# One triangular inverse for two groups of a head, and a planner that counts returns to dense products

## The chip, the cores and the metric

The kernel runs on one core of a Trainium2 chip. Its time is the device time of one execution in microseconds. Five engines work side by side, each in the order that the program gives it: TensorE (PE, with its weight loads as PEld), VectorE (DVE), ScalarE (ACT), GpSimd (POOL) and SyncE (SP), which issues most DMAs. They wait for each other by semaphores.

## The reference

One step of a two-layer model on a prompt of 2048 tokens and on 8 samples of 8 tokens, width 1024, all in float32. Layer 0 multiplies the input by `w_in_even` and feeds two mixers: a gated delta rule of 4 heads (128 x 128 states) and window attention of 8 heads. Layer 1 multiplies by `w_in_odd` and runs an HGRN2 recurrence of 8 heads. Each layer ends with an output product, a norm and a gated side input (`w_ple_proj`, `w_ple_gate`). What matters here is the delta rule, chunk by chunk:

```python
a_mat = jnp.where(strict, jnp.einsum('nhcid,nhcjd->nhcij', kb, k) * decay, 0.0)
t_inv = lax.linalg.triangular_solve(a_mat + eye, jnp.broadcast_to(eye, a_mat.shape), left_side=True, lower=True)
u = jnp.einsum('nhcij,nhcje->nhcie', t_inv, v * beta[..., None])
w = jnp.einsum('nhcij,nhcjd->nhcid', t_inv, kb * eG[..., None])
```

So each chunk of each head needs the inverse of a unit lower triangular matrix. Then a scan over the chunks carries the state: `v_new = u - w s`, an output, and a new `s`.

## The kernel before, in words

**Work.** The big products (input, output and gate products, called dense here) split each float32 operand into a high and a low part of type float32r and add three products. They have 128 x 128 weights and 256 to 512 columns, and take most of TensorE's time. All else, called side work here, is float32: transposes against the identity, products of 128 x 128, and products on small tiles of the array (32x32, 64x64, 128x32 and so on).

**Layer 0.** The prompt's 16 tiles of 128 tokens are taken in three parts, `GROUPS[0]`: tiles 0-1 (with the samples) and 2-5; 6-9 and 10-11; 12-15. Within a part the work runs head by head (`ORDER`): attention heads and delta heads. For each delta head and each group of tiles, `dense_delta` issues four dense products and starts a `delta_unit`. It computes `delta_core` (norms of keys and queries, decay matrices, the matrix X to be inverted), `inverse`, then the scan, and `rms_out`, which stores the normed output for the output product. A chunk is 128 tokens here, one tile.

**The inverse.** `inverse` works on all tiles of a group at once. Inside the four 32x32 blocks on the diagonal it doubles the size of the inverted blocks in four levels. A level is: VectorE transposes, TensorE multiplies 32x32 tiles (4 a tile of tokens), ScalarE copies the result out of PSUM, TensorE multiplies again, VectorE merges under a mask. Then a join puts the 32-blocks together to 64 (matmuls of one position of the array after the other, for b = 0 and b = 2), and a last one to 128. Each of these steps needs the one before.

**The order.** Every piece of work is a Python generator that yields one instruction at a time. The planner (`Sched.run`, L525) keeps a model clock for each engine; at each turn it takes, of all threads' next instructions, the one that could start first, adds margins (`MARGIN` 700 ns on what TensorE reads) and hands it to its engine. What it writes down is the order on each engine; at run time nothing is reordered. `SWITCH` and `STAY` weigh a change of the array's tile shape: a whole-array matmul is put back by 1000 ns in all while the array is in a small shape. Dense products have the lowest priority of equals (`LATER`) and so fill what the side work leaves. Dense products write three PSUM banks, side work the other five. Since all instructions are recorded in one helper, the profile names line 354 for them all; tiles called `ar` are blocks of on-chip memory, `bank` a PSUM bank, `cst` the constants (the identity among them), `os` the stored outputs. A float32 matmul has two records in the profile, a transpose and a float32r matmul one.

Of the kernel before, what the change touches and what calls it, by code (L numbers as in the profile page):

```python
# [57 lines left out]
SWITCH = {True: 213, False: 100}  # L58
STAY = 1000
# [109 lines left out]
class Op:  # L169
    __slots__ = ("eng", "fn", "cost", "rd", "wr", "tab", "nbytes", "mode", "place", "port")  # L170
# [38 lines left out]
class Sched:  # L209
    def __init__(self, tc):  # L210
        self.tc, self.nc = tc, tc.nc
        self.engines = {e: getattr(tc.nc, e) for e in ("tensor", "vector", "scalar", "gpsimd", "sync")}
        self.clk = dict.fromkeys(self.engines, 0.0)
        self.dma = 0.0
        self.tab = 0
        self.mode, self.place = WHOLE, None
# [131 lines left out]
    def op(self, eng, m, kw):  # L348
# [8 lines left out]
        for k, v in kw.items():  # L357
            if hasattr(v, "ap") and hasattr(v, "offset"):
                if k in ("out", "accum_out", "ap"):
                    wr.append(self.key(v))  # L360
                    if k != "accum_out":
                        out = v
                else:
                    rd.append(self.key(v))
                    if src is None:
                        src = v
        o.rd, o.wr = rd, wr
# [5 lines left out]
        if eng == "tensor":  # L373
# [72 lines left out]
    def emit(self, o, t):  # L446
        o.fn()
        c = o.cost
        if o.eng == "tensor":
            if o.mode == self.mode != WHOLE and o.place != self.place:  # L450
                c = 20 if o.mode[0] == 32 else c / 2 if o.place[1] <= self.place[1] else 14
            self.mode, self.place = o.mode, o.place
# [72 lines left out]
    def run(self):  # L525
        while self.threads:
# [6 lines left out]
            for t in self.threads:  # L533
# [5 lines left out]
                if o.eng == "tensor" and self.mode != o.mode:  # L539
                    s -= SWITCH[o.mode == WHOLE] - STAY * (o.mode == WHOLE)  # L540
# [17 lines left out]
def bank(c="rc"):  # L558
    return Ask("bank", c)
# [18 lines left out]
class Step(Sched):  # L578
    def __init__(self, ctx, tc, a, o):
# [33 lines left out]
        self.xs = {}  # L613
        self.xblocks = 0
# [659 lines left out]
    def delta_core(self, np_, n, cs, q, G4, maskD, small, out, own):  # L1274
# [8 lines left out]
        junk = yield al(128)  # L1283
# [3 lines left out]
        for c in range(n):  # L1287
            yield self.A.activation(out=junk[:np_], in_=psk[:np_, c * 128 : (c + 1) * 128], func=AF.Square, accum_out=ss[:, c : c + 1])
# [3 lines left out]
        for c in range(n):  # L1292
            yield self.A.activation(out=junk[:np_], in_=psq[:np_, c * 128 : (c + 1) * 128], func=AF.Square, accum_out=ss[:, n + c : n + c + 1])
        self.freebank(psq)
        self.free(junk)
# [21 lines left out]
        kdb = yield al(WT)  # L1317
# [38 lines left out]
    def inverse(self, np_, n, cs, X, small):  # L1356


        N = X
        nb, w = np_ // 32, n * 32  # L1360
        rows = [slice(32 * r, 32 * r + 32) for r in range(nb)]
        Db = yield al(w)
        Tb = yield al(w)
        Mb = yield al(w)
        Dv, Tv, Mv = (cut(x[:np_], 32) for x in (Db, Tb, Mb))
        for r in range(nb):
            yield self.V.tensor_tensor(out=Dv[rows[r]], in0=X[rows[r], :, rows[r]], in1=bc(self.c("m1")[rows[r]], 1, n), op=ALU.mult)
        yield self.V.tensor_tensor(out=Dv, in0=Dv, in1=bc(self.c("ident32")[:np_], 1, n), op=ALU.add)
        for s in small[1:] + (None,):
            yield self.V.transpose(out=Tb[:np_], in_=Db[:np_])  # L1370
            if s is None:
                break
            pt = yield bank()
            for c in range(n):
                for r in range(nb):
                    p = rows[r]
                    yield self.P.matmul(out=pt[p, c * 32 : c * 32 + 32], lhsT=X[p, c, p], rhs=Tv[p, c, :], start=True, stop=True)
            yield self.A.activation(out=Mb[:np_], in_=pt[:np_, :w], func=AF.Copy)
            for c in range(n):
                for r in range(nb):  # L1380
                    p = rows[r]
# [3 lines left out]
        for r in range(nb):  # L1385
            yield (self.V.tensor_copy(out=N[rows[r], :, rows[r]], in_=Dv[rows[r]]) if r % 2 else self.A.activation(out=N[rows[r], :, rows[r]], in_=Dv[rows[r]], func=AF.Copy))
        if cs == 128:
            pt = yield bank()
            T2b = yield al(n * 64)
            T2 = cut(T2b[:64], 64)  # L1390
            yield self.G.memset(ap=T2b[:64], constant=0.0)
            for b in (0, 2):
                for c in range(n):
# [4 lines left out]
            for b in (0, 2):  # L1398
                for c in range(n):
                    yield self.P.matmul(out=pt[rows[b], w + c * 32 : w + c * 32 + 32], lhsT=Mv[rows[b + 1], c, :], rhs=Dv[rows[b + 1], c, :], start=True, stop=True)  # L1400
            for c in range(n):
                yield self.P.matmul(out=pt[rows[1], 2 * w + c * 32 : 2 * w + c * 32 + 32], lhsT=Dv[rows[1], c, :], rhs=Mv[rows[1], c, :], start=True, stop=True)
            for b in (0, 2):
                yield self.A.activation(out=N[rows[b], :, rows[b + 1]], in_=cut(pt[rows[b], w : 2 * w], 32), func=AF.Copy)
            yield self.V.tensor_copy(out=T2[rows[1], :, 0:32], in_=cut(pt[rows[1], 2 * w : 3 * w], 32))
            self.freebank(pt)
            M2b = yield al(n * 64)
            M2 = cut(M2b[64:128], 64)
            pt = yield bank()
            for c in range(n):  # L1410
                yield self.P.matmul(out=pt[64:128, c * 64 : c * 64 + 64], lhsT=X[0:64, c, 64:128], rhs=T2[:, c, :], start=True, stop=True)
            yield self.A.activation(out=M2b[64:128], in_=pt[64:128, : n * 64], func=AF.Copy)
            for c in range(n):
                yield self.P.matmul(out=pt[0:64, n * 64 + c * 64 : n * 64 + c * 64 + 64], lhsT=M2[:, c, :], rhs=N[64:128, c, 64:128], start=True, stop=True)
            yield self.V.tensor_copy(out=N[0:64, :, 64:128], in_=cut(pt[0:64, n * 64 : 2 * n * 64], 64))
# [4 lines left out]
    def delta_unit(self, half, h, gi, u):  # L1420
# [7 lines left out]
        yield from self.delta_core(128, nt, 128, u["c"], (G[:, sl, h], GmB[:, sl, h], GrB[:, sl, h]), self.c("maskD"), SMALL, r, True)  # L1428
# [36 lines left out]
    def rms_out(self, np_, n, cs, po, lqk, g, sg, dst):  # L1465


        sm = yield al(256)
        f, junk = sm[:np_, 128 : 128 + n], sm[:np_, 0:128]
        for c in range(n):  # L1470
            yield self.A.activation(out=junk, in_=po[:np_, c * 128 : (c + 1) * 128], func=AF.Square, accum_out=f[:, c : c + 1])
# [6 lines left out]
        on = yield al(n * 128)  # L1478
# [237 lines left out]
    def hgrn_core(self, np_, n, cs, q, k, f, deep, out, own):  # L1716
# [14 lines left out]
        def scale(s):  # L1731
# [6 lines left out]
            yield self.V.tensor_tensor(out=qv[:, :, 1, :], in0=qv[:, :, 1, :], in1=bc(bv[:, :, 0], 2, hs), op=ALU.mult)  # L1738
            yield self.V.tensor_tensor(out=kv[:, :, 0, :], in0=kv[:, :, 0, :], in1=bc(bv[:, :, 1], 2, hs), op=ALU.mult)
# [3 lines left out]
            bo += nbk  # L1743
            yield self.V.tensor_tensor(out=B, in0=bv[:, :, 0], in1=bv[:, :, 1], op=ALU.mult)

# [62 lines left out]
        if deep:  # L1808
# [19 lines left out]
            for i, s in enumerate((4, 8, 16)):  # L1828
                yield from level(ps, i * n * 16, s)
            self.freebank(ps)  # L1830
            yield from scale(64)
# [362 lines left out]
```

## Time and profile before

| | |
|---|---|
| median of 3 runs | 3127.14 us (3126.95 to 3135.73) |
| profiled execution | 3119.46 us |
| its span, first to last instruction | 3117.7 us |
| TensorE busy | 3002.6 us (96%) |
| VectorE, ScalarE, GpSimd busy | 1964.8, 1228.3, 198.7 us |
| TensorE idle, ended by VectorE, by ScalarE | 54.3 us, 48.0 us |
| mean granted TensorE clock | 0.983 |
| HBM traffic | 78 GB/s over the span |

The busy time of an engine is the union of its instructions' times. Of TensorE's rows the starts are used, since a matmul's end overlaps the next one's. The span and what lies around it make the profiled execution's own time, which is 7.7 us under the median of the other runs.

### The profile page before, as it was taken

The page shows a single profiled execution, that of the slowest core. Times are in us where ns is not written, and L with a number is a line of the kernel's source. Part 1 is how long each engine was busy: PE and PEld are TensorE (multiplying, and loading weights), DVE is VectorE, ACT ScalarE, POOL GpSimd, SP SyncE. Part 2 cuts the span into 40 slices and gives each one's busy share as a digit, 9 for nine tenths or more (in the row PEclk, how much of TensorE's full clock was granted, in tenths as well). Part 3 has the DMA queues.
Part 4 walks back from the last instruction along what each step waited for, and adds up shares of the span by engine and source line. Part 5 has one row for each costly group of instructions (what it writes and reads, how often), then busy time and mean ns, then how long its engine had stood idle before and what let it go on. Part 6 is the DMA issues. An engine that isn't in the chain of part 4 may idle for free. (4 is left out here: it accounts for less than half of the span.)

```text
span 3117.7 us, 63598 instructions
## 1 busy us (share of the span) xinstructions
PE 3002.6 (96%) x25592; PEld 2498.8 (80%) x25592; DVE 1964.8 (63%) x5693; ACT 1228.3 (39%) x3314; POOL 198.7 (6%) x265
## 2 busy tenths in 40 slices
PE   8999999999999999999999999998999999999999
PEld 7887778877787787878888888887888888787787
DVE  5567776786767675333367786868577677733333
ACT  4555555564556462101144343434444444411011
POOL 0000000000000001111100000000000000111110
PEclk9999999999999999999999999999999999999999
DMA  4221132231214154333332121222221122732331
GB/s 119 71 77 47 47 92 63 71 80 44 68 54 114 48 171 138 87 79 88 88 112 64 49 63 49 76 64 87 70 59 56 44 70 61 213 87 75 83 86 49
DMA packets 320838, 246.45 MB, mean 79 GB/s; under 512 B 33800, under 2 KB 285840, under 8 KB 320528
## 3 DMA queue, kind: packets, MB, share of 16 engines
q1 hardware_dynamic: 253408, 207.80, 22.0%
q0 software_dynamic: 67136, 34.61, 6.2%
q8 instruction: 200, 3.28, 0.4%
q14 instruction: 94, 0.77, 0.1%
HBM read 182.98 MB, written 60.45 MB: 78 GB/s over the span
## 5 line engine op out<-in xcount | busy, mean ns | idle before, releaser
L354 PE MATMUL bank<-ar,ar 128*128 128x512 f32 (+10 forms) x20432 | 2813.2, 302 | 67.2 <-ACT ar L354 39.8
L354 PEld LDWEIGHTS bank<-ar,ar 128*128 128x128 f32 (+4 forms) x20432 | 2244.8, 162 | 474.2 <-ACT ar L354 65.1
L354 ACT ACTIVATE ar<-bank 128x128 f32<-128x128 f32 (+13 forms) x1471 | 525.9, 368 | 1081.5 <-PE bank L354 998.6
L354 DVE TENSOR_TENSOR ar<-ar,ar 128x256 f32<-128x256 f32 (+8 forms) x1500 | 732.6, 517 | 247.9 <-ACT ar L354 210.3
L354 ACT ACTIVATE ar<-ar 128x512 f32<-128x512 f32 (+15 forms) x1067 | 527.8, 522 | 750.0 <-DVE ar L354 384.6
L354 DVE SCALAR_TENSOR_TENSOR ar<-ar,bank 128x512 f32<-128x512 f32 (+3 forms) x256 | 164.1, 641 | 386.6 <-ACT ar L354 254.2
L354 PE MATMUL bank<-cst,ar 128*128 128x128 f32 (+3 forms) x1439 | 239.7, 279 | 27.5 <-DVE ar L354 16.4
L354 PEld LDWEIGHTS bank<-cst,ar 128*128 128x128 f32 (+3 forms) x1439 | 173.5, 141 | 73.8 <-DVE ar L354 16.9
L354 POOL TENSOR_TENSOR ar<-ar,mhalf 128x2 f32<-128x2 f32 (+3 forms) x104 | 109.2, 1050 | 1496.8 <-DVE ar L354 1130.1
L354 DVE TENSOR_TENSOR ar<-bank,ar 128x128 fp32r<-128x128 f32 (+7 forms) x326 | 147.2, 455 | 75.7 <-ACT ar L354 43.7
L354 DVE TENSOR_TENSOR ar<-ar 128x4 f32<-128x4 f32 (+10 forms) x592 | 139.9, 250 | 19.9 <-ACT ar L354 13.3
L354 DVE SCALAR_TENSOR_TENSOR ar<-bank,ar,ar 128x509 f32<-128x509 f32 (+8 forms) x216 | 122.7, 573 | 25.8 <-ACT ar L354 24.4
L354 DVE SCALAR_TENSOR_TENSOR ar<-ar,ar,bank 128x128 f32<-128x128 f32 x192 | 65.8, 343 | 115.2 <-PE bank L354 114.6
L354 PEld LDWEIGHTS bank<-ar 32*32 32x32 f32 (+3 forms) x2640 | 88.8, 121 | 38.9 <-ACT ar L354 13.6
L354 PE MATMUL bank<-ar 32*32 32x32 f32 (+5 forms) x2640 | 113.7, 209 | 4.5 <-ACT ar L354 2.3
L354 DVE COPY_PREDICATED ar<-cst,bank 128x64 f32<-128x64 uint32 (+3 forms) x356 | 85.9, 242 | 34.9 <-PE bank L354 24.4
L354 DVE SCALAR_TENSOR_TENSOR ar<-ar,ar,ar 128x1024 f32<-128x1024 f32 (+1 forms) x68 | 87.0, 1280 | 13.8 <-POOL ar L354 13.8
L354 POOL MEMSET ar<- 128x256 f32 (+4 forms) x85 | 29.1, 348 | 961.1 <-PE bank L354 550.6
L354 DVE SCALAR_TENSOR_TENSOR ar<-ar,ar 128x4 f32<-128x4 f32 (+10 forms) x190 | 58.4, 312 | 31.7 <-ACT ar L354 30.5
L354 POOL DMA_DIRECT2D ar<-os x64 | 57.3, 898 | 296.9 <-PE bank L354 197.0
L354 ACT ACTIVATION_READ_ACCUMULATOR ar<-bank 128x1 f32 (+1 forms) x340 | 66.2, 195 | 0.0
L354 ACT ACT_TABLE_LOAD x49 | 62.9, 1283 | 5.5 <-DVE ar L354 4.0
(55 smaller groups left out, 799.9 us busy)
## 6 DMA issues: line engine op xcount, KB each, us to landing
ar<-os POOLq DMA_DIRECT2D x64, 512.0 KB, 5.0
ar<-in_w_in_odd SPq DMA_DIRECT2D x64, 512.0 KB
ar<-in_w_in_even SPq DMA_DIRECT2D x60, 512.0 KB
os<-ar SPq DMA_DIRECT2D x36, 512.0 KB
ar<-x SPq DMA_DIRECT2D x32, 512.0 KB
os<-ar SPq DMA_DIRECT2D x56, 256.0 KB
ar<-in_x_prompt SPq DMA_DIRECT2D x16, 512.0 KB
ar<-in_w_ple_gate SPq DMA_DIRECT2D x16, 512.0 KB
```

The lines of the kernel that those rows point to most:

```text
L354: o.fn = lambda: f(**kw)
```

## The change

It has four parts.

- **The meeting.** Where a part has two groups, the unit of the first group that has its X waits (in the planner, as a condition of its generator) until the second has its own; that one's thread then runs one `inverse` over the tiles of both and lets the first go on. With 2 and 4 tiles a phase has 24 small matmuls instead of 8 and 16.
- **The join** issues the matmuls of both halves (b = 0 and 2) before the two ScalarE copies, and in turn by position; results that went to three stretches of the bank go to two.
- **The planner** counts 90 ns for the first dense product behind anything else (`BACK`), puts a dense product back by 300 ns when the last instruction on TensorE was other whole-array work, and by 900 ns in all (before, 1000) when the array is in a small shape.
- **Scrap results apart.** The squares on ScalarE, of which only the sums are used, write to separate columns of a tile that is filled later. In layer 1 the scalings and the merges under masks are recorded in turn.

```diff
-SWITCH = {True: 213, False: 100}
-STAY = 1000
+SWITCH = {True: 105, False: 120}
+BACK = 90
+STAY = (900, 300)
...
+            o.dense = o.mode == WHOLE and m != "transpose" and kw["rhs"].dtype == F32R
...
+            if o.dense and not self.was_dense:
+                c += BACK
+            self.mode, self.place, self.was_dense = o.mode, o.place, o.dense
...
-                if o.eng == "tensor" and self.mode != o.mode:
-                    s -= SWITCH[o.mode == WHOLE] - STAY * (o.mode == WHOLE)
+                if o.eng == "tensor":
+                    if self.mode != o.mode:
+                        s -= SWITCH[o.mode == WHOLE] - STAY[0] * (o.mode == WHOLE)
+                    elif o.dense and not self.was_dense:
+                        s += STAY[1]
...
-        yield from self.inverse(np_, n, cs, X, small)
+        if own:
+            yield from self.meet(own, X, np_, cs, small)
+        else:
+            yield from self.inverse(np_, cs, [X], small)
...
+    def meet(self, own, X, np_, cs, small):
+
+        m = self.met.setdefault(own, [])
+        m.append(X)
+        if len(m) < len(GROUPS[0][own[0]]):
+            yield until(lambda: own not in self.met)
+            return
+        yield from self.inverse(np_, cs, m, small)
+        del self.met[own]
+        self.dirty = True
...
+            for c, (X, i) in enumerate(at):
+                for b in (0, 2):
+                    yield self.P.matmul(out=pt[rows[b + 1], c * 32 : c * 32 + 32], lhsT=X[rows[b], i, rows[b + 1]], rhs=Tv[rows[b], c, :], start=True, stop=True)
             for b in (0, 2):
-                for c in range(n):
-                    yield self.P.matmul(out=pt[rows[b + 1], c * 32 : c * 32 + 32], lhsT=X[rows[b], c, rows[b + 1]], rhs=Tv[rows[b], c, :], start=True, stop=True)
-                yield self.A.activation(out=Mb[rows[b + 1]], in_=pt[rows[b + 1], :w], func=AF.Copy)
+                yield self.A.activation(out=Mb[rows[b + 1], :w], in_=pt[rows[b + 1], :w], func=AF.Copy)
...
-            yield self.A.activation(out=junk, in_=po[:np_, c * 128 : (c + 1) * 128], func=AF.Square, accum_out=f[:, c : c + 1])
+            yield self.A.activation(out=on[:np_, c * 128 : (c + 1) * 128], in_=po[:np_, c * 128 : (c + 1) * 128], func=AF.Square, accum_out=f[:, c : c + 1])
```

How it moves the instructions, at two places on TensorE. First a level of the first delta head's inverse: its two phases on 32x32 tiles and what stands between them. Before, for the group of two tiles (`bank_73` takes the small results, `bank_68` a dense product's):

```order
L354 MATMUL bank_73<-ar_2203,ar_1790 32x32 x8
L354 MATMUL bank_68<-ar_123,ar_2016 128x320
L354 MATMUL bank_68<-ar_124,ar_2015 128x320
L354 MATMUL bank_68<-ar_127,ar_2015 128x320
L354 MATMUL bank_68<-ar_124,ar_2016 128x320
L354 MATMUL bank_68<-ar_124,ar_2015 128x320
L354 MATMUL bank_68<-ar_127,ar_2015 128x320
L354 MATMUL bank_68<-ar_124,ar_2016 128x320
L354 MATMUL bank_73<-ar_2203 32x32 x8
```

Of the change, for both groups (`bank_70` takes the small results; `ar_118` and `ar_2415` are the two groups' X):

```order
L355 MATMUL bank_70<-ar_2312,ar_118 32x32 x8
L355 MATMUL bank_70<-ar_2312,ar_2415 32x32 x16
L355 MATMUL bank_67<-ar_182,ar_1911 128x512
L355 MATMUL bank_67<-ar_183,ar_1910 128x512
L355 MATMUL bank_67<-ar_187,ar_1910 128x512
L355 MATMUL bank_67<-ar_183,ar_1911 128x512
L355 MATMUL bank_67<-ar_183,ar_1910 128x512
L355 MATMUL bank_70<-ar_2312 32x32 x24
```

The 8 and 16 small matmuls of two levels now stand together, with five dense products of 512 columns between the phases where seven of 320 stood.

Second the join's first step, with the semaphores that each row waits for. Before, for a group of four tiles: half b = 0, half b = 2, then dense products, then the second step:

```order
L354 MATMUL bank_71<-ar_2432,ar_2522 32x32 [waits DVE_49]
L354 MATMUL bank_71<-ar_2432,ar_2522 32x32 x3
L354 MATMUL bank_71<-ar_2432,ar_2522 32x32 [waits Activation_49]
L354 MATMUL bank_71<-ar_2432,ar_2522 32x32 x3
L354 MATMUL bank_68<-ar_181,ar_2016 128x512
L354 MATMUL bank_68<-ar_182,ar_2015 128x512
L354 MATMUL bank_68<-ar_186,ar_2015 128x512
L354 MATMUL bank_68<-ar_182,ar_2016 128x512
L354 MATMUL bank_68<-ar_182,ar_2015 128x512
L354 MATMUL bank_71<-ar_2359,ar_2432 32x32 [waits Activation_49]
```

Of the change, for both groups together, up to the first dense products:

```order
L355 MATMUL bank_69<-ar_2312,ar_118 32x32 [waits DVE_49]
L355 MATMUL bank_69<-ar_2312,ar_118 32x32 x3
L355 MATMUL bank_69<-ar_2312,ar_2415 32x32 x8
L355 MATMUL bank_68<-ar_184,ar_1951 128x512
L355 MATMUL bank_68<-ar_188,ar_1951 128x512
L355 MATMUL bank_68<-ar_184,ar_1952 128x512
L355 MATMUL bank_66<-ar_181,ar_2217 128x512
```

The wait for ScalarE between the halves is gone: the twelve matmuls stand together, and the next row that waits for ScalarE is the second step, 16 dense products later.

More of the change, by code (lines that the diff above doesn't have):

```diff
@@ L169 @@
 class Op:
-    __slots__ = ("eng", "fn", "cost", "rd", "wr", "tab", "nbytes", "mode", "place", "port")
+    __slots__ = ("eng", "fn", "cost", "rd", "wr", "tab", "nbytes", "mode", "place", "port", "dense")
 class Ask:
@@ L215, in __init__ @@
         self.tab = 0
-        self.mode, self.place = WHOLE, None
+        self.mode, self.place, self.was_dense = WHOLE, None, True
         self.port = 0.0
@@ L613, in __init__ @@
         self.xs = {}
+        self.met = {}
         self.xblocks = 0
@@ L1364, in inverse @@
         Mb = yield al(w)
[L1365 to L1367 removed]
+        Dv, Tv, Mv = (cut(x[:np_, :w], 32) for x in (Db, Tb, Mb))
+        for X, g in groups:
+            for r in range(nb):
+                yield self.V.tensor_tensor(out=Dv[rows[r], g], in0=X[rows[r], :, rows[r]], in1=bc(self.c("m1")[rows[r]], 1, g.stop - g.start), op=ALU.mult)
         yield self.V.tensor_tensor(out=Dv, in0=Dv, in1=bc(self.c("ident32")[:np_], 1, n), op=ALU.add)
         for s in small[1:] + (None,):
[L1370 removed]
+            yield self.V.transpose(out=Tb[:np_, :w], in_=Db[:np_, :w])
             if s is None:
@@ L1373, in inverse @@
             pt = yield bank()
+            for c, (X, i) in enumerate(at):
+                for p in rows:
+                    yield self.P.matmul(out=pt[p, c * 32 : c * 32 + 32], lhsT=X[p, i, p], rhs=Tv[p, c, :], start=True, stop=True)
+            yield self.A.activation(out=Mb[:np_, :w], in_=pt[:np_, :w], func=AF.Copy)
             for c in range(n):
[L1375 to L1378, printed above, removed]
-            for c in range(n):
-                for r in range(nb):
-                    p = rows[r]
+                for p in rows:
                     yield self.P.matmul(out=pt[p, w + c * 32 : w + c * 32 + 32], lhsT=Mv[p, c, :], rhs=Dv[p, c, :], start=True, stop=True)
@@ L1396, in inverse @@
+        if cs == 128:
             for r in range(2):
                 yield self.V.tensor_copy(out=T2[rows[r], :, rows[r]], in_=Tv[rows[r]])
-            for b in (0, 2):
-                for c in range(n):
-                    yield self.P.matmul(out=pt[rows[b], w + c * 32 : w + c * 32 + 32], lhsT=Mv[rows[b + 1], c, :], rhs=Dv[rows[b + 1], c, :], start=True, stop=True)
             for c in range(n):
-                yield self.P.matmul(out=pt[rows[1], 2 * w + c * 32 : 2 * w + c * 32 + 32], lhsT=Dv[rows[1], c, :], rhs=Mv[rows[1], c, :], start=True, stop=True)
@@ L1403, in inverse @@
-            for b in (0, 2):
-                yield self.A.activation(out=N[rows[b], :, rows[b + 1]], in_=cut(pt[rows[b], w : 2 * w], 32), func=AF.Copy)
-            yield self.V.tensor_copy(out=T2[rows[1], :, 0:32], in_=cut(pt[rows[1], 2 * w : 3 * w], 32))
+                k = slice(w + c * 32, w + c * 32 + 32)
+                for b in (0, 2):
+                    yield self.P.matmul(out=pt[rows[b], k], lhsT=Mv[rows[b + 1], c, :], rhs=Dv[rows[b + 1], c, :], start=True, stop=True)
+                yield self.P.matmul(out=pt[rows[1], k], lhsT=Dv[rows[1], c, :], rhs=Mv[rows[1], c, :], start=True, stop=True)
@@ L1406, in inverse @@
+            pv = cut(pt[:, w : 2 * w], 32)
+            yield self.V.tensor_copy(out=T2[rows[1], :, 0:32], in_=pv[rows[1]])
+            for X, g in groups:
+                for b in (0, 2):
+                    yield self.A.activation(out=X[rows[b], :, rows[b + 1]], in_=pv[rows[b], g], func=AF.Copy)
             self.freebank(pt)
             M2b = yield al(n * 64)
-            M2 = cut(M2b[64:128], 64)
+            M2 = cut(M2b[64:128, : n * 64], 64)
             pt = yield bank()
-            for c in range(n):
-                yield self.P.matmul(out=pt[64:128, c * 64 : c * 64 + 64], lhsT=X[0:64, c, 64:128], rhs=T2[:, c, :], start=True, stop=True)
@@ L1412, in inverse @@
[L1412 to L1415, printed above, removed]
+            for c, (X, i) in enumerate(at):
+                yield self.P.matmul(out=pt[64:128, c * 64 : c * 64 + 64], lhsT=X[0:64, i, 64:128], rhs=T2[:, c, :], start=True, stop=True)
@@ L1416, in inverse @@
+            yield self.A.activation(out=M2b[64:128, : n * 64], in_=pt[64:128, : n * 64], func=AF.Copy)
+            for c, (X, i) in enumerate(at):
+                yield self.P.matmul(out=pt[0:64, c * 64 : c * 64 + 64], lhsT=M2[:, c, :], rhs=X[64:128, i, 64:128], start=True, stop=True)
+            for X, g in groups:
+                yield self.V.tensor_copy(out=X[0:64, :, 64:128], in_=cut(pt[0:64, : n * 64], 64)[:, g])
             self.freebank(pt)
```

53 lines of the change are left out of this document (30 added, 23 removed).

## The prediction

> **What bounds the kernel now.** I read the page first, its busy times and its slices.
>
> ```profile
> span 3117.7 us, 63598 instructions
> PE 3002.6 (96%) x25592; PEld 2498.8 (80%) x25592; DVE 1964.8 (63%) x5693; ACT 1228.3 (39%) x3314; POOL 198.7 (6%) x265
> PE   8999999999999999999999999998999999999999
> PEclk9999999999999999999999999999999999999999
> ```
>
> TensorE is busy for 96% of the span in every slice but two; no other engine comes near. So a gain must come out of TensorE's own time: fewer or cheaper matmuls, less lost between them, or part of the 115 us in which it is idle. The windows by stage, and the waits of TensorE, say where the idle time is (columns of the windows: length, then busy time and instructions of each engine, granted clock, DMA share, GB/s).
>
> ```profile
> 0.00:1143.00 1143.00, 1072.54 (x10732) 883.43 (x10732) 787.71 (x2621) 619.58 (x1745) 32.02 (x62) 0.97 0.27 76
> 1143.00:1600.00 457.00, 452.33 (x2128) 365.93 (x2124) 206.13 (x359) 83.79 (x176) 50.21 (x48) 1.00 0.40 105
> 2180.00:2205.00 25.00, 20.04 (x118) 15.39 (x117) 12.64 (x45) 9.37 (x36) 1.25 (x2) 0.73 0.45 139
> PE bank L354 <- DVE ar L354: 54.3, 92, 3.1
> PE bank L354 <- ACT ar L354: 48.0, 46, 7.3
> ```
>
> The first 1143 us, where attention and the delta rule run beside layer 0's input products, hold 70 of the 115 us. The change works in that stretch.
>
> **What a switch of TensorE costs.** The number of matmuls of each shape is the same in both programs (19,344 in all, counted in both orders), so the products themselves give nothing. What changes is who stands beside whom. I took the price of a neighbour from the timeline of TensorE, by the starts, because the ends overlap. First, transposes between dense products of 128x512:
>
> ```profile
> 1213.95 0.60 PE L354 MATMUL bank<-cst,ar 128*128 128x128 f32 x4
> 1214.31 1.40 PE L354 MATMUL bank<-ar,ar 128*128 128x512 f32 x5
> 1215.54 0.60 PE L354 MATMUL bank<-cst,ar 128*128 128x128 f32 x4
> 1215.90 23.65 PE L354 MATMUL bank<-ar,ar 128*128 128x512 f32 x103
> 1239.38 0.60 PE L354 MATMUL bank<-cst,ar 128*128 128x128 f32 x4
> ...
> 103.74 1.25 PE L354 MATMUL bank<-cst,ar 128*128 128x128 f32 x10
> 104.75 0.77 PE L354 MATMUL bank<-ar,ar 128*128 128x384 f32 x3
> ```
>
> 103 dense matmuls take 23.48 us from start to start and 5 take 1.23, so one takes 0.227 and the return to dense adds 0.095. But four transposes take 0.36 and ten 1.01: one takes 0.108, four should take 0.43, and 0.07 is given back, since the last one is followed early. A return from transposes, and likewise from whole-array float32 products, costs some 0.02 us net. That is not the 90 ns that the changed planner charges as BACK.
>
> Small tiles are another matter:
>
> ```profile
> 677.85 0.45 PE L354 MATMUL bank<-ar 32*32 32x32 f32 x32 [0.20 <-DVE ar L354]
> 678.24 1.42 PE L354 MATMUL bank<-ar,ar 128*128 128x512 f32 x5
> 679.59 0.45 PE L354 MATMUL bank<-ar 32*32 32x32 f32 x32
> 679.97 1.65 PE L354 MATMUL bank<-ar,ar 128*128 128x512 f32 x6
> ...
> 239.16 0.33 PE L354 MATMUL bank<-ar 32*32 32x32 f32 x16
> 239.42 1.29 PE L354 MATMUL bank<-ar,ar 128*128 128x320 f32 x7
> ```
>
> Each float32 matmul has two records. The 5 dense ones between two small phases take 1.35 us, 0.215 over 5 x 0.227. A phase of 16 small matmuls takes 0.38, one of 8 takes 0.26: 0.016 a matmul and 0.13 fixed. **An excursion from dense to small tiles and back costs 0.215 + 0.13 = 0.345 us besides its matmuls.**
>
> **The change part by part.**
>
> *One inverse for two groups.* Layer 0's part 0 and part 1 have two groups a head, part 2 has one. So 20 inverses over groups of 2 or 4 tiles become 12 (eight of 6 tiles, four of 4), and the two of the samples stay. Over the whole order, excursions away from the whole array fall from 430 to 352, runs of 32x32 from 199 to 124: 78 x 0.345 = **-27 us**.
>
> *Positions in turn.* In the join of the 32-blocks the order before issues the matmuls of all tiles at one position of the array, then those of the next; now positions alternate.
>
> ```profile
> 281.23 0.43 PE L354 MATMUL bank<-ar,ar 32*32 32x32 f32 x8
> 748.46 0.21 PE L354 MATMUL bank<-ar,ar 32*32 32x32 f32 x1 [3.09 <-ACT ar L354]
> ```
>
> Four at one position take 0.43 with their tail, as long as the sixteen above (0.45); the tail alone is 0.21. That is 0.055 each against 0.016. The order before has 221 neighbours at one position, the changed one none: 221 x 0.04 = **-9 us**.
>
> These rows give -36. As a second way I took the median distance from start to start for each kind of neighbours (the shape before, the shape, the shape behind) over all of TensorE's records, and summed it along both orders: 2919 us before, 2870 after, **-49**. The rest of the second sum is dense matmuls that stood alone between other work (116 before, 6 now) and switches from one small shape to another. The lower bound is -27, were the positions hidden and the rest nothing. I take **-48**, near the finer count.
>
> *The wait inside the join goes.* ScalarE's rows of two such places, with TensorE's, and the groups of 32x32 matmuls (columns: busy, mean ns, idle before and what ended it):
>
> ```profile
> 745.85 1.28 ACT L354 ACT_TABLE_LOAD   x1
> 747.14 0.30 ACT L354 ACTIVATE ar<-ar,eps 128x4 f32<-128x4 f32 x1
> 747.43 0.69 ACT L354 ACTIVATE ar<-bank,ar 128x512 f32<-128x512 f32 x1
> 748.14 0.27 ACT L354 ACTIVATE ar<-bank 32x128 f32<-32x128 f32 x1
> ...
> 283.15 1.32 PE L354 MATMUL bank<-ar,ar 32*32 32x32 f32 x11 [1.49 <-ACT ar L354]
> 283.62 0.27 ACT L354 ACTIVATE ar<-bank 32x128 f32<-32x128 f32 x1 [0.52 <-PE bank L354]
> ...
> L354 PE MATMUL bank<-ar,ar 32*32 32x32 f32 x3752 | 75.8, 196 | 29.5 <-ACT ar L354 20.8 <-DVE ar L354 8.6
> L354 PE MATMUL bank<-ar 32*32 32x32 f32 x1048 | 20.0, 198 | 2.3 <-ACT ar L354 1.7 <-DVE ar L354 0.2
> ```
>
> The second half of the first join writes the bank that ScalarE still reads for the first half, and nothing stands between the halves. At 748.46 TensorE had waited 3.09 us, because ScalarE had a table load and two other instructions to do first. I count 18 such places, 22 us together, which are nearly all of the 20.8 + 1.7 that ScalarE ended in these groups. Now both halves come first and both copies behind them, with dense work until the next phase: **-22 us**. Next in line is ScalarE's copy for the second phase; if its cover failed, as many waits of 0.5 to 1 us would be back in 12 places, 6 to 12 us.
>
> *New waits.* The rule that charges 300 for a return from other whole-array work makes the planner take a side matmul that is up to 0.3 us late, so its margin of 0.7 us shrinks to 0.4. I priced the TensorE work between the cause of each awaited ScalarE or VectorE result and its user, by the same medians. Before, 24 uses have under 0.4 us of it (the joins and a few more), now 4. Between 0.4 and 1.1 us there are 32 before and 62 now. In the run before those 32 lost 7 us together, 0.22 each; 30 more are **+5 us**, a little less than 30 x 0.22, as most of them lie above 0.9. The bounds: 0, and +41, were each of 136 returns 0.3 us late (returns to dense fall from 1014 to 800, of which 78 are the excursions above).
>
> *At nothing.* The meeting is a condition of the planner: no engine waits in it. The first group's scan, norm and store are only recorded later, on SP's queue too; their reader is the output product behind the last head. ScalarE loses 56 copies, VectorE some 100 small instructions; at 39% and 63% they are hidden, as are the squares that now write apart and the other order of scalings in layer 1. If the cover were gone, they would count as gains.
>
> Sum: -48 - 22 + 5 = **-65 us**, so 3119.46 becomes 3054 for a profiled execution. The profiled one lies 7.7 us under the median of the runs, 3127.14: **3062 us**.
>
> **The rivals.**
>
> *Phases exposed (slower).* Two inverses that ran side by side covered each other's round trips; one inverse has 8 + 3 of them, 132 in the 12. From 283.15 to the end of ScalarE's copy at 283.89 is 0.74 us. All exposed they are +98, so 3160; from 88 exposed on nothing is gained, from about 100 it is slower. For it: one place of the changed order has only four whole-array products between two phases. Against it: most have four to ten dense ones of 0.227.
>
> *Clock (slower).* The granted clock is 1.00 where dense products run through and 0.73 in the window at 2180, where mixed work and waits stand. Over the span 0.017 of the clock is missing, 53 us; the clock records have it in 16 stretches at half clock, so 6.6 us long on average, each losing 3.3.
>
> ```profile
> core 0: 3117.7 us, clock 0.983
> ```
>
> By the order, stretches over 2 us without a dense product rise from 20 to 43. If each of the 23 new ones brought a half-clock stretch it would cost 23 x 3.3 = 76 us: 3138. Against it: those over 3.4 us rise only from 7 to 10, which would be 10 us. The Trainium skill ("TensorE: Matmul & The Clock Gate", Part 4: PE-mode transpose) says that transposes do not count as activity for the clock, which speaks against bunching them. The trace fits it at 2180 and cannot tell it from the waits there.
>
> *Only the wait goes (faster, less).* The excursions' price is won on TensorE and lost to later results, since the planner's durations and the chip's differ and each reordering finds new late ones: 3127 - 22 - 10 = 3095, to 3115.
>
> *More.* Fewer waits also mean less of the 53 us of missing clock, and the uses that had 1.5 us and more of cover fall too: another 15 to 30, so 3040.
>
> **How the numbers follow.** Forecast (3040 to 3085) 0.60; more (under 3040) 0.15; only the wait (3085 to 3117) 0.17; phases exposed 0.04; clock 0.04. The range of 8 in 10 leaves out the slower cases and the best tail: 3035 to 3100. A change within 0.3% (9 us) can't be told from none; of the 0.08 of the two slower cases 0.03 ends there: faster 0.92, same 0.03, slower 0.05.
>
> **What would show it.** In the changed profile: the row of 32x32 matmuls with under 10 us ended by ScalarE instead of 20.8; TensorE's idle time in layer 0 down from 70 to about 50; excursions at the same 0.345; the clock at 0.98. It is wrong if waits for VectorE or ScalarE before whole-array matmuls grow by over 30 us, or if the granted clock falls to 0.96.

## The result and the profile after

The changed kernel takes **3048.68 us** (median of 4 runs, 3046.65 to 3053.54) against 3127.05 us for the kernel before: ratio 0.9746, 95% interval 0.9724 to 0.9767. Forecast were 3062 us and a range of 3035 to 3100. The profiled execution took 3046.65 us, its span 3044.4 us.

The page of the changed kernel, its busy times and clock slices:

```profile
span 3044.4 us, 63289 instructions
PE 2947.7 (97%) x25592; PEld 2477.3 (81%) x25592; DVE 1947.0 (64%) x5589; ACT 1202.0 (39%) x3258; POOL 195.6 (6%) x257
PEclk9989999999999999999999999998999999999999
```

Its clock, in the view of the cores:

```profile
core 0: 3044.4 us, clock 0.987
```

TensorE has the same 25592 records and 54.9 us less busy time; the span is 73.3 us shorter. The windows of layer 0 (columns as before: length, busy time and instructions of PE, PEld, DVE, ACT, POOL, clock, DMA share, GB/s), cut where its part on 32x32 tiles now ends:

```profile
0.00:1090.00 1090.00, 1033.78 (x10766) 867.96 (x10766) 778.23 (x2538) 601.04 (x1696) 30.61 (x54) 0.98 0.29 79
1090.00:1540.00 450.00, 446.76 (x2077) 361.42 (x2076) 199.37 (x334) 78.66 (x164) 51.08 (x48) 1.00 0.40 106
```

TensorE is idle for 56.2 us there, where it was 70.5 us in the longer window before (about 50 was expected). The waits of TensorE, and its two groups of 32x32 matmuls:

```profile
PE bank L355 <- DVE ar L355: 53.1, 81, 5.1
PE bank L355 <- ACT ar L355: 20.0, 19, 7.5
PE bank L355 <- DMA ar<-x: 10.2, 2, 5.5
```

```profile
L355 PE MATMUL bank<-ar,ar 32*32 32x32 f32 x3860 | 55.5, 195 | 7.7 <-DVE ar L355 5.5 <-ACT ar L355 1.3 <-DVE halo L355 0.6
L355 PE MATMUL bank<-ar 32*32 32x32 f32 x940 | 15.3, 194 | 1.9 <-issue 1.9
```

What ScalarE ended fell from 48.0 to 20.0 us; of the 20.8 + 1.7 us before 32x32 matmuls 1.3 are left. Neither VectorE's waits nor the clock got worse; the two waits for a load of x grew, from 4.5 to 10.2 us, and some 3 us of small waits are new.

The price of an excursion is what it was. TensorE's timeline in layer 0's last part, then two rows from an earlier place:

```profile
948.34 0.45 PE L355 MATMUL bank<-ar 32*32 32x32 f32 x32
948.73 1.65 PE L355 MATMUL bank<-ar,ar 128*128 128x512 f32 x6
950.22 0.60 PE L355 MATMUL bank<-cst,ar 128*128 128x128 f32 x4
...
952.57 1.18 PE L355 MATMUL bank<-ar,ar 128*128 128x512 f32 x4
953.67 0.45 PE L355 MATMUL bank<-ar 32*32 32x32 f32 x32
...
679.05 0.62 PE L355 MATMUL bank<-ar,ar 32*32 32x32 f32 x48
679.60 0.44 PE L355 MATMUL bank<-cst,ar 128*128 128x128 f32 x2
```

Sixteen small matmuls take 0.39 us from start to start and six dense ones behind them 1.49, which is 0.13 over 6 x 0.227: the way back. On the way out, four dense ones between transposes and a small phase take 1.10, 0.19 over 4 x 0.227, of which 0.095 is the return from the transposes. Together that is 0.225, where the prediction had 0.215. (Over all stretches of 128x512 products between two small phases, without waits and at full clock, the median is 0.226 now and 0.223 before.) A phase for both groups, 24 matmuls (48 records), takes 0.55: with the same fixed 0.13, 0.0175 a matmul.

**Where the time went.** I set the start-to-start medians of the kernel before, by kind of neighbours, against the starts of the changed one. TensorE's first to last start went from 3104.5 to 3029.9 us. Of these 74.6 us, 49.4 are neighbours (2919.3 to 2869.9) and 25.3 what lies over the medians (185.2 to 159.9). The first of these is counted along the order with the old medians, as in the prediction; only the total is measured. By place: layer 1's scan begins 55.4 us earlier, as the first of its 128x16 matmuls shows, before and after:

```profile
1640.51 0.45 PE L354 MATMUL bank<-ar 128*32 128x16 f32 x32
```

```profile
1585.10 0.44 PE L355 MATMUL bank<-ar 128*32 128x16 f32 x32
```

From there to its last such matmul it takes 1019.5 us instead of 1032.4, and the rest 432.8 instead of 438.9.

### The profile page after: what moved, and what is told of

The parts are those of the page before. It is cut to its first block, busy times and chain, and to the rows that moved or that the text cites. A ratio compares the mean times of both kernels' runs of the same rounds, so it can differ in the third digit from the quotient of the medians.

```text
span 3044.4 us, 63289 instructions
## 1 busy us (share of the span) xinstructions
PE 2947.7 (97%) x25592; PEld 2477.3 (81%) x25592; DVE 1947.0 (64%) x5589; ACT 1202.0 (39%) x3258; POOL 195.6 (6%) x257
## 5 line engine op out<-in xcount | busy, mean ns | idle before, releaser
L355 PE MATMUL bank<-ar,ar 128*128 128x512 f32 (+9 forms) x20370 | 2752.3, 300 | 59.3 <-DVE ar L355 37.4
L355 PEld LDWEIGHTS bank<-ar,ar 128*128 128x128 f32 (+3 forms) x20370 | 2227.1, 161 | 436.6 <-issue 53.8
L355 ACT ACTIVATE ar<-bank 128x128 f32<-128x128 f32 (+12 forms) x1415 | 514.3, 378 | 1105.5 <-PE bank L355 1027.0
L355 DVE TENSOR_TENSOR ar<-ar,ar 128x128 f32<-128x128 f32 (+11 forms) x1494 | 748.8, 520 | 247.2 <-ACT ar L355 204.2
L355 ACT ACTIVATE ar<-ar 128x256 f32<-128x256 f32 (+12 forms) x1061 | 527.5, 524 | 669.4 <-DVE ar L355 309.9
L355 PE MATMUL bank<-cst,ar 128*128 128x128 f32 (+2 forms) x1439 | 236.0, 280 | 21.7 <-DVE ar L355 10.4
L355 PEld LDWEIGHTS bank<-cst,ar 128*128 128x128 f32 (+2 forms) x1439 | 171.7, 141 | 68.0 <-DVE ar L355 14.4
L355 POOL TENSOR_TENSOR ar<-ar,mhalf 128x2 f32<-128x2 f32 (+4 forms) x104 | 106.7, 1026 | 1586.3 <-DVE ar L355 1140.2
L355 DVE TENSOR_TENSOR ar<-ar 128x128 f32<-128x128 f32 (+9 forms) x598 | 139.3, 248 | 18.1 <-ACT ar L355 14.7
L355 PEld LDWEIGHTS bank<-ar 128*32 128x32 f32 (+3 forms) x2702 | 86.0, 120 | 30.1 <-issue 16.4
```

Of the source, the lines that this page charges most:

```text
L355: o.fn = lambda: f(**kw)
```

## The experiments

"Start of layer 1" is the time of that first 128x16 matmul in the profiled execution, "scan" the length of its stage, "neighbours" the sum of the old medians along the order, and "over" what TensorE's time from first to last start has beyond that sum. Each ratio is against runs of the kernel before in the same session, whose medians lie between 3125.62 and 3132.48 us.

| kernel | median us | ratio (95%) | start of layer 1 | scan | neighbours | over |
|---|---|---|---|---|---|---|
| before | 3127.05 | 1 | 1640.5 | 1032.4 | 2919 | 185 |
| the change | 3048.68 | 0.9746 (0.9724 to 0.9767) | 1585.1 | 1019.5 | 2870 | 160 |
| the change, again | 3053.15 | 0.9754 (0.9734 to 0.9773) | 1588.5 | 1024.1 | 2870 | 168 |
| new join alone | 3100.39 | 0.9911 (0.9896 to 0.9926) | 1620.9 | 1034.0 | 2908 | 180 |
| planner alone | 3133.11 | 1.0011 (0.9995 to 1.0027) | 1638.2 | 1045.8 | 2916 | 195 |
| planner of before | 3078.77 | 0.9837 (0.9819 to 0.9855) | 1591.3 | 1042.3 | 2872 | 191 |
| no meeting | 3086.99 | 0.9866 (0.9847 to 0.9884) | 1625.0 | 1025.2 | 2902 | 175 |
| returns free | 3042.90 | 0.9732 (0.9716 to 0.9749) | 1573.7 | 1026.6 | 2871 | 157 |
| old first join step | 3071.42 | 0.9820 (0.9803 to 0.9837) | 1606.0 | 1023.4 | 2875 | 180 |
| scrap, layer 1 as before | 3086.41 | 0.9869 (0.9852 to 0.9886) | 1609.4 | 1036.7 | 2877 | 194 |
| scrap alone as before | 3073.44 | 0.9822 (0.9802 to 0.9841) | 1603.6 | 1027.1 | 2874 | 182 |
| margin 720 | 3063.62 | 0.9796 (0.9779 to 0.9813) | 1585.5 | 1035.9 | 2872 | 175 |
| leaving free | 3105.12 | 0.9919 (0.9903 to 0.9936) | 1603.8 | 1056.8 | 2906 | 179 |
| leaving at 2000 | 3197.35 | 1.0209 (1.0189 to 1.0229) | 1710.7 | 1034.7 | 2838 | 335 |

### The join

The kernel before with the new `inverse` for one group, nothing else:

```diff
-        yield from self.inverse(np_, n, cs, X, small)
+        yield from self.inverse(np_, cs, [X], small)
```

> The kernel before with the new join alone: both halves of the first step ahead of the two copies, positions in turn; every group keeps its own inverse, the planner and all else are as before. Theory (TensorE's time is the sum of neighbour prices plus the waits that have no cover): the neighbour sum along this order is 2908 us against 2919 (positions, -9), and uses with under 0.4 us of cover fall from 24 to 5, worth 22 us. So about 3092 us, -35, and the 32x32 groups lose under 5 us to ScalarE instead of 22. Rival 'excursions carry it all, the waits come back elsewhere': 3115 to 3120.

27 us, 8 fewer than the theory and nearer to it than to the rival. The 32x32 groups lose 3.2 us to ScalarE, as expected. Its waits of TensorE:

```profile
PE bank L354 <- DVE ar L354: 61.5, 91, 3.3
PE bank L354 <- ACT ar L354: 33.1, 31, 7.4
```

ScalarE's fell by 14.9 us from 48.0, and VectorE's rose by 7.2 from 54.3: about half of the wait that went came back as another. The reverse, the change with the old first step of the join:

```diff
             for b in (0, 2):
+                for c, (X, i) in enumerate(at):
+                    yield self.P.matmul(out=pt[rows[b + 1], c * 32 : c * 32 + 32], lhsT=X[rows[b], i, rows[b + 1]], rhs=Tv[rows[b], c, :], start=True, stop=True)
                 yield self.A.activation(out=Mb[rows[b + 1], :w], in_=pt[rows[b + 1], :w], func=AF.Copy)
```

> The changed kernel with the first step of the join as before: the matmuls of one half, ScalarE's copy, then the other half; meeting, planner, scrap and layer 1 as changed. So 12 merged inverses wait again in their join (16 uses under 0.4 us of cover instead of 4), and the matmuls of a half stand at one position (104 such neighbours instead of 0; neighbour sum 2875 against 2870). Theory: 12 x 1.2 us = +14 and +5, layer 1 as in the changed kernel, since the order there is the same: 3066 to 3070, and the first small matmul of layer 1 at 1600 to 1605. Rival 'the wait is hidden, since VectorE's next result is late anyway': 3049 to 3056.

It costs 23 us, nearly all ahead of layer 1 (1606.0 against 1585.1). In its profile part of the wait is back, in what ScalarE ended in all and before the 32x32 group:

```profile
PE bank L355 <- ACT ar L355: 31.2, 31, 7.6
L355 PE MATMUL bank<-ar,ar 32*32 32x32 f32 x4340 | 68.8, 196 | 14.0 <-ACT ar L355 8.5 <-DVE ar L355 4.0 <-DVE halo L355 0.6
```

By TensorE's starts the two halves stand apart in twelve places again, by 0.61 to 1.64 us, 9 us together where the theory had 14. With the 5 of the neighbours that is 14 of the 23; the rest was not traced.

### The meeting

```diff
-        if own:
-            yield from self.meet(own, X, np_, cs, small)
-        else:
-            yield from self.inverse(np_, cs, [X], small)
+        yield from self.inverse(np_, cs, [X], small)
```

> The changed kernel in which each group keeps its own inverse (20 instead of 12); join, planner, scrap and layer 1 as changed. Excursions 435 instead of 352, neighbour sum 2902 against 2870, waits without cover the same (5 and 4 uses under 0.4 us). Theory: 31 us slower than the changed kernel, 3080. Rival 'the waits in the join were the gain and merging only moves work': 3049 to 3055. Rival of the other sign 'merging exposes phases': under 3049.

38 us are lost, and layer 1 starts 40 us later: the meeting is the largest part. The profiled executions lie 46 apart; of that the neighbours give 31 (435 excursions instead of 352) and what lies over the medians 15.

### The planner's numbers

Two kernels: the one before with the new numbers and rules alone, and the change with the old numbers. The diff is the second's:

```diff
-SWITCH = {True: 105, False: 120}
-BACK = 90
-STAY = (900, 300)
+SWITCH = {True: 213, False: 100}
+BACK = 0
+STAY = (1000, 0)
```

> The kernel before with the planner's new numbers and rules alone (SWITCH, BACK, STAY); inverses, join and all else as before. Returns to dense fall from 1014 to 876, excursions to small tiles stay at 434 (430 before). Theory: a return from whole-array side work costs 0.02 us net, so 138 fewer give 3 us; the neighbour sum along this order is 2916 against 2919; five waits less in joins by chance. 3117 to 3127. Rival 'each return costs the 90 ns that the planner charges': -12 from the returns beside that, so 3105 to 3115.

> The changed kernel with the planner's numbers and rules of before (returns to dense cost nothing there, small shapes are held as before); meeting, join, scrap and layer 1 as changed. Returns to dense 930 instead of 800, excursions 365 instead of 352, neighbour sum 2872 against 2870 of the changed kernel. Theory: 3050 to 3057, within 0.3% of the changed kernel's 3049. Rival '90 ns a return': 130 x 0.09 = +12, 3060 or more.

Alone they are worth nothing (1.0011, interval across 1). With the meeting, the old numbers gave 3078.77, 30 us over the change, where 3050 to 3057 was expected: a miss. But up to layer 1, where the meeting is, only 6 us differ; 23 stand in layer 1's scan. Is that the numbers' doing, or that of any other order? Two more orders tell. One changes only the margin on what TensorE reads (`MARGIN = 720` instead of 700):

> The changed kernel with one number of the planner moved a little: MARGIN 720 instead of 700. It means nothing by itself and gives another order, so it measures what a new order alone does. Neighbour sum 2872 against 2870; 6 uses under 0.4 us against 4, 38 under 1.1 against 62. Theory: within 10 us of the changed kernel up to layer 1 (1575 to 1595) and within 20 in all, 3040 to 3070. If it lies over 3070, single comparisons of 20 us between orders say nothing.

Layer 1 starts at the same time and its scan is 16 us longer. So a change of 20 ns in a margin, which means nothing by itself, moves that stage by 16 of those 23 us, and the 30 us say little about the numbers. The other lets the returns go free:

```diff
-BACK = 90
-STAY = (900, 300)
+BACK = 0
+STAY = (900, 0)
```

> The changed kernel in which the planner counts nothing for a return to dense from whole-array side work (BACK 0, second STAY 0); its other numbers and all else as changed. Returns to dense rise from 800 to 940, excursions stay (354 and 352), the neighbour sum is 2871 against 2870. The runs so far showed that layer 1's waits change by some 20 us with any new order, so two readings: the start of layer 1's first small matmul (1585 us in the changed kernel) and the total. Theory (a return costs 0.02 net): the first at 1582 to 1592, since 59 returns more up to there cost 1 us; layer 1 loses 10 to 25 as it did with the planner of before; total 3050 to 3075. Rival '90 ns a return': 59 x 0.09 = +5 up to there and +7 behind, plus the same: 1590 or more and over 3065. Rival 'the planner's counting is worth nothing in layer 1 either': 3046 to 3053.

With 940 returns to dense instead of 800 it takes 3042.90, the least of all, and layer 1 starts at 1573.7: both lie below every reading written down beforehand. The price for returns, the part of the change that gives its description "counts returns to dense products", buys nothing. Whether leaving it out gains is open: 0.9732 stands against 0.9746 and 0.9754. The expectation of the repeated run (below) would call that a little better, but the intervals overlap, and a new order alone moved more (0.9796 with margin 720).

The change has one more line, which its four parts do not name: the planner now counts the target of a masked merge (`copy_predicated`) as read. No run undid it alone; "new join alone" and "planner alone" are without it.

### The scrap results

The prediction had put the squares at nothing. First the squares and the layer 1 order as before, then the squares alone:

```diff
-            yield self.A.activation(out=kdb[:np_, c * 128 : (c + 1) * 128], in_=psk[...], func=AF.Square, accum_out=ss[:, c : c + 1])
+            yield self.A.activation(out=junk[:np_], in_=psk[...], func=AF.Square, accum_out=ss[:, c : c + 1])
...
-            yield self.A.activation(out=on[:np_, c * 128 : (c + 1) * 128], in_=po[...], func=AF.Square, accum_out=f[:, c : c + 1])
+            yield self.A.activation(out=junk, in_=po[...], func=AF.Square, accum_out=f[:, c : c + 1])
```

> The changed kernel with the squares written to one scrap tile again and layer 1's scalings and merges in the order of before; meeting, join and planner as changed. Neighbour sum 2877 against 2870, waits without cover about the same (5 and 4 uses under 0.4 us, 48 and 62 under 1.1). Theory (these edits are hidden behind TensorE): up to layer 1's first small matmul as in the changed kernel, 1580 to 1592; layer 1 within 5 of the changed kernel's 1452 if the planner alone made its -19 there, 10 to 30 more if it takes both. Totals 3050 to 3057 or 3060 to 3080. Rival 'ScalarE's squares held up the heads': up to layer 1 over 1600.

> The change, but only the squares go back to one scrap tile per head (in the step of the delta rule and in the norm of the output); the order of scalings in layer 1 stays as changed. The undoing of all of the rest together gave 3086, with layer 1 starting at 1609 us instead of 1585. Theory: the squares that write one scrap tile wait for each other on ScalarE, and this holds up the start of heads; then layer 1 starts at 1600 to 1612 us, the groups of 32x32 matmuls show 10 us or more that VectorE or ScalarE ended, and the time is 3060 to 3085. Rival: the scrap tiles are worth nothing and the 24 us of that run came with its new order; then layer 1 starts at 1583 to 1592 us and the time is 3045 to 3065.

Both runs speak against "nothing", and the first lies above both readings of its theory. The squares alone cost 20 us against the change in the same comparison (0.9822 against 0.9754, intervals apart), 15 of them ahead of layer 1; the other 13 to 15 us of the first run lie in the range that a new order moves by itself. The 15 do not: the five orders with meeting, new join and separate tiles (the change twice, planner of before, returns free, margin 720) start layer 1 at 1573.7 to 1591.3, the two with one tile at 1603.6 and 1609.4. The reason stands in ScalarE's timeline. Before, a square and the read of its sum, then the next:

```profile
657.29 0.28 ACT L354 ACTIVATE ar<-bank 128x128 f32<-128x128 f32 x1
657.46 0.20 ACT L354 ACTIVATION_READ_ACCUMULATOR ar<-bank 128x1 f32 x1
657.69 0.28 ACT L354 ACTIVATE ar<-bank 128x128 f32<-128x128 f32 x1
657.86 0.20 ACT L354 ACTIVATION_READ_ACCUMULATOR ar<-bank 128x1 f32 x1
...
658.26 0.20 ACT L354 ACTIVATION_READ_ACCUMULATOR ar<-bank 128x1 f32 x1
658.35 0.47 ACT L354 ACTIVATE ar<-bank,ar 128x256 f32<-128x256 f32 x1
```

The changed kernel:

```profile
637.48 0.28 ACT L355 ACTIVATE ar<-bank 128x128 f32<-128x128 f32 x1 [0.31 <-PE bank L355]
637.66 0.20 ACT L355 ACTIVATION_READ_ACCUMULATOR ar<-bank 128x1 f32 x1
637.75 0.27 ACT L355 ACTIVATE ar<-bank 128x128 f32<-128x128 f32 x1
637.91 0.20 ACT L355 ACTIVATION_READ_ACCUMULATOR ar<-bank 128x1 f32 x1
638.00 0.28 ACT L355 ACTIVATE ar<-bank 128x128 f32<-128x128 f32 x1
```

And with one scrap tile in the changed kernel:

```profile
642.65 0.28 ACT L355 ACTIVATE ar<-bank 128x128 f32<-128x128 f32 x1
642.82 0.19 ACT L355 ACTIVATION_READ_ACCUMULATOR ar<-bank 128x1 f32 x1
643.05 0.28 ACT L355 ACTIVATE ar<-bank 128x128 f32<-128x128 f32 x1
```

Squares into one tile follow each other by 0.40 us, squares into tiles of their own by 0.25 to 0.27 (medians over some 200 such pairs in each kernel: 0.399, 0.250, 0.400). A square that writes where the last one wrote waits for it on ScalarE's own semaphore (216 of 229 such pairs before; in the change 174 of 228 wait for nothing). It starts 0.23 after the start of the read of the sum and not 0.09, and the gap is so short that the rows show no idle time for it. The Trainium skill ("ScalarE: Activation LUTs", What ACT_TABLE_LOAD costs) says that back-to-back activations overlap by about 93 ns. The rows of the changed kernel are near that: an instruction starts 0.10 to 0.11 us before the one ahead has ended. With one tile the square starts 0.03 to 0.04 after the end of the read, so the wait on the engine's own result takes the overlap away. With four tiles a head has eight squares ahead of its X, 1.2 us.

That these 1.2 us are what TensorE then waits for is argued, and only partly shown. TensorE's waits with one scrap tile, and in the second run of the change beside it:

```profile
PE bank L355 <- DVE ar L355: 62.9, 99, 5.3
PE bank L355 <- ACT ar L355: 30.3, 25, 7.4
```

```profile
PE bank L355 <- DVE ar L355: 54.2, 81, 5.1
PE bank L355 <- ACT ar L355: 24.2, 24, 7.6
```

They differ by 14.8 us, the neighbours by 4.5, which is most of the 20. Ahead of layer 1 TensorE is idle for 79.8 us with one tile and for 68.4 in that run of the change.

### Leaving the whole array

The planner puts a whole-array matmul back by 900 ns while the array is in a small shape. Once nothing, once 2000:

```diff
-STAY = (900, 300)
+STAY = (0, 300)
```

> The change with nothing charged for leaving the whole array: 585 excursions instead of 352, 143 runs of 32x32 matmuls instead of 124. Theory with the price of the prediction, 0.345 us an excursion: 233 more are +80, so 3129. Rival, the price summed over neighbours (2906.7 against 2870.2): +36, so 3085, 0.16 an excursion, because most of the new ones are single matmuls of other small tiles and not phases of 32x32. Either may be up to 20 us off by the new order in layer 1; layer 1 starts at 1585 plus the share of layer 0.

> The change with 2000 instead of 900 charged for leaving the whole array: 228 excursions instead of 352, 38 runs of 32x32 matmuls instead of 124, but 110 instead of 4 uses of a result with under 0.4 us of TensorE's work ahead of them. By the neighbours alone it gains 32 us (2838.5 against 2870): 3017. Theory (a phase of small tiles has to be covered by dense work, about 0.74 us from its last matmul to the end of ScalarE's copy, less the fixed tail): some 106 uncovered results at 0.4 to 1.2 us each are 42 to 127 us, so 3060 to 3145, likeliest 3100 to 3140. Rival (excursions are what counts, round trips are mostly hidden by what stands already in the queues): under 3045.

At nothing, 233 excursions more cost 52 us against the change beside it, 47 by the spans: 0.20 each. So 0.345 is too much and the rival's 0.16 too little. 0.345 is the price between dense products on both sides; most of the new excursions are not such (141 of the 233 lie in layer 1's scan, where the neighbours price them at 27.7 us, 0.20 each, and the scan took 32.7 longer than in the second run of the change, 0.23 each). What the neighbours miss is not waits of a size that the profile shows. Its waits, and its busy times:

```profile
PE bank L355 <- DVE ar L355: 52.4, 76, 5.1
PE bank L355 <- ACT ar L355: 23.1, 21, 7.4
```

```profile
PE 3008.4 (97%) x25592; PEld 2498.8 (81%) x25592; DVE 1946.6 (63%) x5589; ACT 1195.4 (39%) x3258; POOL 194.7 (6%) x257
```

The two waits are 75.5 us here and 78.4 in the second run of the change, while TensorE's busy time is 56.5 us longer (2951.9 there): the old medians price the new neighbours too low, by 11 us of the 47. Why was not tried.

At 2000 the rival of the prediction that phases come to stand exposed came true. The neighbours fall by 32 us and the time rises by 144, past the kernel before and past the 3060 to 3145 of the theory, which did not count the clock. TensorE's timeline, its waits, the window and the clock of that kernel:

```profile
719.65 0.62 PE L355 MATMUL bank<-ar,ar 32*32 32x32 f32 x48 [1.39 <-DVE ar L355]
720.70 0.62 PE L355 MATMUL bank<-ar,ar 32*32 32x32 f32 x48 [0.43 <-ACT ar L355]
...
726.19 0.62 PE L355 MATMUL bank<-ar,ar 32*32 32x32 f32 x48 [0.43 <-ACT ar L355]
727.74 0.62 PE L355 MATMUL bank<-ar,ar 32*32 32x32 f32 x48 [0.94 <-DVE ar L355]
728.85 0.86 PE L355 MATMUL bank<-ar,ar 32*32 32x32 f32 x48 [0.49 <-ACT ar L355]
730.67 0.87 PE L355 MATMUL bank<-ar,ar 32*32 32x32 f32 x48 [0.96 <-DVE ar L355]
```

```profile
PE bank L355 <- DVE ar L355: 107.9, 134, 4.9
PE bank L355 <- ACT ar L355: 67.6, 85, 7.6
```

```profile
728.70:735.00 6.30, 3.72 (x170) 3.25 (x171) 2.58 (x10) 0.61 (x3) 0.00 (x0) 0.50 0.01 3
```

```profile
core 0: 3186.5 us, clock 0.955
```

With nothing dense between the phases each waits 0.43 to 0.49 us for ScalarE's copy or 0.94 to 0.96 for VectorE's merge and transpose. Then the clock halves and the same 24 matmuls take 0.86. TensorE's waits for the two engines grow by 102 us against the change; missing clock grows from 40 us (0.013 x 3044) to 143 (0.045 x 3186). The two overlap (30 of the 143 us fall on idle time), so what lies over the medians grows by less than the sum of both, by 175 us.

And the change itself again, beside these three:

> The change itself once more, beside the three others and the same runs of the kernel before: 3046 to 3054, so that the version with free returns (3042.9, 0.9732 of before) can be told from it or not: if it is 0.9740 or more of before again, free returns are a little better; if 0.9735 or less, no difference.

It took 3053.15 us (0.9754), within what was expected.

## Why the prediction was right

**Of the 13 us between 3062 and 3048.7, 6 are the frame.** The sum was 3054 for a profiled execution and 7.7 were added for the median. The profiled execution took 3046.65, but lay only 2.0 under its median. Against its own kind the sum missed by 7.8.

**Switches, -48.** The way was right, the size some 10 us too large. The -49.4 above does not test it, being the same count along the same orders. A measure apart from it is TensorE's busy time for the same matmuls, 54.9 us less. Part of that is the clock: by the clock records, half-clock stretches lengthened busy time by 46 us before and by 29 now (half of TensorE's busy time inside them), so 38 us are left, an estimate. By the same measure taking out the meeting loses 27 (31 by neighbours) and the new join alone gains 8 (11). Of the two ways of counting, 36 and 49, the coarser came nearer to it.

**What made up for it.** TensorE's span fell by 73.3 us: those 38, another 17 of busy time that the faster clock gave, and 18.4 of idle time (-22 + 5 = -17 were forecast). The sum had nothing for the clock; the prediction named it only under "More". And the excursions and the join lie ahead of layer 1's scan, yet 19.0 of the 74.6 us came behind its start. That the total missed by only 8 is in part luck.

**The join's wait, -22.** Its rows went as written (20.8 + 1.7 to 1.3). Alone it did not bring all of it, as half came back behind VectorE; inside the whole change, undoing it costs 23 with its positions, of which 9 are seen as this wait.

**New waits, +5.** Not seen in the change: 62 uses have 0.4 to 1.1 us of cover, but VectorE's waits stayed (54.3, 53.1) and ScalarE's fell by 28.0 instead of 22. A use short of the margin is not a late one. With the planner's rules alone, though, VectorE's waits rose to 71.2 us while ScalarE's fell to 37.9, so the term is not shown to be wrong.

**Meeting at nothing, returns at nothing.** Nothing speaks against either: no wait of size appeared with the meeting; counting returns bought nothing by itself (1.0011), and making them free lost nothing (0.9732).

**A reading.** "Busy for 96% of the span in every slice but two" is not what the slices say: they show 90% or more, and 96% is the mean of the whole span. Nothing in the sum hangs on it.

**The squares at nothing: the step that failed.** "ScalarE loses 56 copies ...; at 39% and 63% they are hidden, as are the squares that now write apart". They are worth 20 us. The share of busy time said that ScalarE has room, but the squares stand in a chain, ahead of a head's X, and their cost was not in the busy time. (That the chain is what TensorE waits for is partly shown, as said above.) The row was in the trace before: the read of the last sum is followed after 0.09 us, those between squares after 0.23. The total hides this: the join added alone, and the meeting and the squares taken out alone, come to 27 + 38 + 20 = 85 us where the whole gave 78, and the switches brought less than counted. So the gain that was left out stood in for others; this too is luck.

**The rivals.** The clock rose (0.983 to 0.987), though stretches without a dense product doubled in the order: a stretch without dense work is not an idle one. The Trainium skill ("TensorE: Matmul & The Clock Gate", Part 4: PE-mode transpose) says that transposes do not count as activity; it did not decide here. The Trainium skill ("TensorE: Matmul & The Clock Gate", Part 1: The HAM clock gate) has the clock go by windows of 3.4 us; the clock records agree, with half-clock stretches of 3.4, 6.8 and 10.2 us. At 2000 the clock halved behind a run of short waits of which none was over 1.4 us (rows above), so no single wait as long as a window was needed. Whether the share of idle time did it or the lack of dense work in the same microseconds, these rows do not separate. Exposed phases did not come at a weight of 900 and came at 2000, so that rival hangs on the planner's weight for leaving the whole array.

**Left open.** Why layer 1's scan takes anything from 1020 to 1046 us in orders whose neighbours there differ by less than 10 was not tried. About half of the difference is TensorE's idle time in that stage: 23.5 us in the change, 30.6 with margin 720, 34.5 with the planner of before, 39.8 with the planner alone. A difference of under 20 us in that stage proves nothing about the edit.

## What to carry to other kernels

Price switches of the array by its neighbours in the trace, over the whole order, and keep dense work between two dependent small phases: in the change fewer switches gained 38 to 49 us with such cover, and a further 32 by neighbours cost 144 net without it. Before putting an instruction "at nothing" because its engine is idle for half the time, look at the distance from its start to the next one's: a scrap result that is never read still orders its writers. And test a planner's parts one by one beside a run with a trifling change of order; here that alone moved the time by 0.5%.

## What was not expected of the hardware

- ScalarE's squares with a sum follow each other by 0.40 us into one scrap tile and by 0.25 into tiles of their own; the 0.15 shows in no idle column.
- Behind a run of small phases with waits of 0.4 to 1.4 us between them TensorE's clock halved (0.50 from 728.7 to 735.0 us).
- Three times the matmuls in a phase on 32x32 tiles only double its time: 8, 16 and 24 take 0.26, 0.38 and 0.55 us.
